# Later due times for part of the scaled inputs in the builder of a planned transformer block

## The chip, the cores and the metric

The kernel runs on one core of a Trainium2 chip. A core has TensorE (PE, matrix products into the PSUM banks), VectorE (DVE), ScalarE (ACT), GpSimd (POOL) and SyncE (SP, which issues most of the loads from memory). Each engine works through its own list of instructions in order and waits on semaphores for the others. The metric is device microseconds of one execution, as a median of runs.

## The reference

One block of a network on 256 tokens of width 2048, in float32: a gated feed-forward network (FFN), a mixer, and a second FFN, each between two RMS norms. Only the FFN matters here:

```python
def _rmsnorm(x, g):
    xf = x.astype(jnp.float32)
    y = xf * lax.rsqrt(jnp.mean(xf * xf, axis=-1, keepdims=True) + NORM_EPS)
    return (y * g.astype(jnp.float32)).astype(x.dtype)

def _swiglu(x, w_gate, w_up, w_down):
    return (jax.nn.silu(x @ w_gate) * (x @ w_up)) @ w_down
...
h = x
f = _swiglu(_rmsnorm(h, ln_ffn1_pre[l]), ffn1_gate[l], ffn1_up[l], ffn1_down[l])
h = h + MACARON_WEIGHT * _rmsnorm(f, ln_ffn1_post[l])
mx = _hybrid_mixer(...)
h = h + _rmsnorm(mx, ln_mix_post[l])
f = _swiglu(_rmsnorm(h, ln_ffn2_pre[l]), ffn2_gate[l], ffn2_up[l], ffn2_down[l])
h = h + MACARON_WEIGHT * _rmsnorm(f, ln_ffn2_post[l])
```

The hidden width of the FFN is 5632.

## The kernel before

**Products in three parts.** A float32 value v is kept as a high part H (a ScalarE cast to the type fp32r) and a low part L = v - H (a VectorE subtraction); `split` (line 651) makes both. A product of two such values is three matmuls, H.H, H.L and L.H (`mm3`, line 670). So each weight tile `w` that arrives needs a cast `wH` on ScalarE and a subtraction `wL` on VectorE before TensorE may use it. A weight pair is two k-tiles of 128 rows by 512 columns in one tile of 128x1024; it feeds 12 matmuls. There are five buffers each for `w`, `wH` and `wL`, given out in the order of the program; more are borrowed from 36 general units.

**Blocks of an FFN.** The 5632 hidden columns are worked in 11 blocks of 512, each with a gate half (banks `f`) and an up half (banks `l`), over 16 k-tiles of the input. Block 0 (banks `mm`) starts before the norm is known: it uses the raw input, and the norm is applied behind it. After block 0 `normed` (line 1221) makes the scaled inputs for blocks 2 and later. The input is held transposed in four quarters, i = 0 to 3, each of four k-tiles (128x1024). For each quarter `normed` does a multiplication by the norm's factors (in the first FFN in place, `xT<-xT,rsb`, after four column scalings `xT<-xT,cols` on ScalarE; in the second FFN `nx<-nx,rsb`, after an addition `nx<-xH,xL`), a `split` into `xH` and `xL`, and, for the first three quarters, `sums` (line 726): four small VectorE operations into `sf`, and a split of it into `sH` and `sL`. Block 1 still uses the raw input.

**Strassen-like blocks.** In blocks 2 to 10 some pairs of k-tiles ("quads", four or five of a block, from the first k-tiles on) are computed by a scheme with seven products in place of eight, which needs sums of inputs (`sums`) and sums of weights (VectorE: `t<-w,w`, `w<-w,t`). The first four products of each quad of block b + 1 (`early`, line 938) are woven into block b (`block_seq`, line 1088). In block 1 the first of them comes after seven of the eight gate pairs. It reads the first quarter; block 2's four quads read the first and second quarter and their sums; block 2's own pairs begin with the third quarter; the sums of the third quarter serve the fifth quad of block 3.

**The builder.** The program is recorded as a list of operations, and `Plan` (line 133) orders it: `deadlines` (line 292) gives each operation a due time, and `simulate` (line 328) plays the engines with modelled durations. Whenever an engine is free, it takes the ready operation with the earliest due time, or, if that one cannot get a buffer, the next. TensorE keeps the order of the program within each of its streams. The order that results is what is emitted. An operation is recorded with `nom`, the sum of the modelled times of the main matmuls recorded ahead of it, and with `lag`, 12000 ns unless something sets it:

```python
d = o.nom + (0.0 if o.eng == "PE" else o.lag) + soon.get(o.i, 0.0) * EASE
for x in o.succs:
    if o.eng == "PE" and x.eng == "PE":
        continue
    e = x.dl - o.dur - SYNC - (2500 if o.nbytes else 0)
    ...
    if e < d:
        d = e
o.dl = d
```

So an operation is due at its place in the program plus its lag, or a little before its earliest reader is due, whichever comes first. A matmul is due at its place; a weight low, therefore, just before its first matmul. All of `normed` is recorded between blocks 0 and 1, and so has the `nom` of the start of block 1.

In the profile nearly every instruction carries line 543, where the builder emits; instructions are told apart by the names of their tiles.

Of the kernel before, what the change touches and what calls it, by code (L numbers as in the profile page):

```python
# [88 lines left out]
NCOL = sum(n for _, n in COLS)  # L89
ONES = 8  # L90
FIRST = 0.4


class Op:
# [462 lines left out]
class Block:  # L557
# [68 lines left out]
    def raw(s, own=False):  # L626
        if own:
            return s.unit(p="w32")
        return s.tile(s.wp, [P, 1024], F32, "w32", "w32", W32_BUFS)
# [456 lines left out]
class Kernel(Block):  # L1086

    def block_seq(s, J, N, ev):
# [14 lines left out]
        if N and N.quads:  # L1103
            n, m = len(N.quads), len(own)
            a = FIRST if J.quads == [] else 0.0
            pos = [round((a + (1 - a) * (i + 0.5) / n) * (m - 3)) for i in range(n)]
# [114 lines left out]
    def normed(s, uT, rb, su, most, raw=None):  # L1221
        nc = s.nc
        V = nc.vector
        nT = s.new_T(len(uT))
        fl = lambda t: t.rearrange("p k t -> p (k t)")
        for i in range(len(uT)):
            (uH, uL), (nH, nL) = uT[i], nT[i]
            if raw:
                x = raw(i)
            else:  # L1230
                x = s.unit((P, 4, S), F32, "nx")
                with s.set(behind=s.late):
                    V.tensor_tensor(out=fl(x), in0=fl(uH).bitcast(F32),
                                    in1=fl(uL).bitcast(F32), op=ALU.add)
            V.tensor_tensor(out=x, in0=x, in1=rb.unsqueeze(1).to_broadcast([P, 4, S]),
                            op=ALU.mult)
            s.split(fl(x), fl(nH), fl(nL))
            if i < (most + 1) // 2:
                s.sums(x.rearrange("p (a b) (h t) -> p a b h t", a=2, h=2), su)
        return nT  # L1240

    def down(s, wd, at, KT, ev, raws, plan, q0=0, acc=()):
# [1039 lines left out]
```

## Time and profile before

| | |
|---|---|
| median of 3 runs | 1980.72 us (1979.87 to 1981.63) |
| the profiled execution | 1982.55 us |
| its span, first to last instruction | 1980.9 us |
| mean granted TensorE clock | 0.998 |
| busy: PE, DVE, ACT, POOL | 1967.8, 1828.3, 1279.1, 179.1 us |
| HBM read, written | 472.59 MB, 27.13 MB |

All times in the views count from the first instruction. A timeline row is start, duration, engine, line, operation, out<-in, shapes and count; in brackets the engine's idle time before it and what ended that. A matmul's duration is longer than its step to the next one, since matmuls are pipelined: the pace is read from the starts. A windows row gives a stretch, its length, the busy time (and instruction count) of PE, PEld, DVE, ACT and POOL, the granted clock, the DMA share and GB/s. A waits row is who waited for whom, the total in us, how many times, and the longest.

### The profile page before, as it was taken

The numbers are of one execution on the slowest core, as the hardware profiler recorded it, in microseconds if no ns is written. First come the engines' busy times: TensorE is split into PE (matmuls) and PEld (weight loads), VectorE is DVE, ScalarE is ACT, GpSimd is POOL, SyncE is SP. The second block draws the span as 40 slices with busy tenths as digits, with TensorE's granted clock in tenths as the row PEclk, the third lists the DMA queues.
The fourth block names the chain that finished last, engine by engine and source line by source line (L and its number), as shares of the span: only waits on it lengthen the run. The fifth ranks groups of instructions, "written<-read, shape, count | busy, mean of one in ns | idle before, by whom it ended". The sixth has DMA issues, their size and how long they took to land.

```text
span 1980.9 us, 28671 instructions
## 1 busy us (share of the span) xinstructions
PE 1967.8 (99%) x9650; PEld 1625.8 (82%) x9650; DVE 1828.3 (92%) x2313; ACT 1279.1 (65%) x1664; POOL 179.1 (9%) x260
## 2 busy tenths in 40 slices
PE   9999999999999999999999999999999999999998
PEld 7788888888888888888888788888888888888886
DVE  7999999999999988999799779998999999999996
ACT  8567767666655657764665465576667676766563
POOL 0111111100001020001400100011101111000000
PEclk9999999999999999999999999999999999999999
DMA  9899999987769788758566498778999999877684
GB/s 322 251 306 281 290 296 294 296 283 229 241 203 294 245 254 281 219 166 256 171 209 180 120 324 269 228 262 245 298 277 298 285 298 285 282 238 232 215 288 144
DMA packets 278163, 502.69 MB, mean 254 GB/s; under 512 B 25472, under 2 KB 53888, under 8 KB 278016
## 3 DMA queue, kind: packets, MB, share of 16 engines
q1 hardware_dynamic: 257360, 460.08, 70.1%
q0 software_dynamic: 20224, 40.38, 10.5%
q8 instruction: 76, 1.25, 0.2%
q14 instruction: 71, 0.58, 0.1%
q10 hardware_dynamic: 432, 0.40, 0.1%
HBM read 472.59 MB, written 27.13 MB: 252 GB/s over the span
## 4 chain that ended last, share of the span: by engine, by line
PE 59%; DVE 2%; ACT 1%; issue 1%; DMA 0%; POOLq 0%; ACTq 0%; DVEq 0%
PE l L543 18%; PE mm L543 18%; PE f L543 16%; PE p L543 4%; DVE wL L543 1%; PE pY L543 0%; PE pA L543 0%; ACT wH L543 0%; PE pU L543 0%; DVE AR L543 0%; PE pSa L543 0%; DVE BK L543 0%; PE mc L543 0%; PE pg L543 0%; PE pM L543 0%
## 5 line engine op out<-in xcount | busy, mean ns | idle before, releaser
L543 ACT CAST wH<-w 128x1024 fp32r<-128x1024 f32 (+2 forms) x730 | 749.8, 1043 | 450.3 <-PE mm L543 96.0
L543 DVE TENSOR_TENSOR wL<-w,wH 128x1024 fp32r<-128x1024 f32 (+2 forms) x730 | 870.3, 1208 | 89.1 <-ACT wH L543 76.1
L543 PE MATMUL l<-wL,xH 128*128 128x512 f32 x814 | 316.9, 389 | 0.2 <-DVE wL L543 0.2
L543 PE MATMUL l<-wH,xL 128*128 128x512 f32 x814 | 316.7, 389 | 0.0
L543 PE MATMUL l<-wH,xH 128*128 128x512 f32 x814 | 316.7, 389 | 0.0
L543 PE MATMUL mm<-wL,xH 128*128 128x512 f32 (+1 forms) x568 | 220.2, 388 | 1.3 <-DVE wL L543 1.3
L543 PE MATMUL mm<-wH,xH 128*128 128x512 f32 (+1 forms) x568 | 221.0, 389 | 0.2 <-ACT xH L543 0.2
L543 PE MATMUL mm<-wH,xL 128*128 128x512 f32 (+1 forms) x568 | 219.1, 386 | 0.0
L543 PE MATMUL f<-wL,xH 128*128 128x512 f32 x552 | 216.1, 392 | 2.9 <-DVE wL L543 2.9
L543 PE MATMUL f<-wH,xL 128*128 128x512 f32 x552 | 216.0, 391 | 0.0
L543 PE MATMUL f<-wH,xH 128*128 128x512 f32 x552 | 215.8, 391 | 0.0
L543 ACT CAST wH<-t 128x1024 fp32r<-128x1024 f32 (+1 forms) x166 | 169.4, 1020 | 62.5 <-DVE t L543 25.7
L543 DVE TENSOR_TENSOR wL<-t,wH 128x1024 fp32r<-128x1024 f32 (+1 forms) x166 | 195.9, 1180 | 5.9 <-ACT wH L543 4.8
L543 PEld LDWEIGHTS l<-wL,xH 128*128 128x128 f32 x814 | 152.8, 188 | 32.3 <-DVE wL L543 0.7
L543 PEld LDWEIGHTS l<-wH,xH 128*128 128x128 f32 x814 | 152.8, 188 | 31.7
L543 PEld LDWEIGHTS l<-wH,xL 128*128 128x128 f32 x814 | 152.8, 188 | 31.6
L543 DVE TENSOR_TENSOR t<-w,w 128x1024 f32<-128x1024 f32 (+1 forms) x112 | 134.4, 1200 | 1.4 <-DMA w<-in_w_in_dram 0.4
L543 PEld LDWEIGHTS mm<-wL,xH 128*128 128x128 f32 x568 | 106.9, 188 | 22.4 <-DVE wL L543 2.0
L543 PEld LDWEIGHTS mm<-wH,xH 128*128 128x128 f32 x568 | 106.7, 188 | 22.3 <-ACT xH L543 0.6
L543 PEld LDWEIGHTS f<-wL,xH 128*128 128x128 f32 x552 | 104.3, 189 | 25.0 <-DVE wL L543 3.3
L543 PEld LDWEIGHTS mm<-wH,xL 128*128 128x128 f32 x568 | 106.7, 188 | 20.5
L543 PEld LDWEIGHTS f<-wH,xH 128*128 128x128 f32 x552 | 104.3, 189 | 21.8
(324 smaller groups left out, 3095.7 us busy)
## 6 DMA issues: line engine op xcount, KB each, us to landing
w<-in_ffn_gate_dram SPq DMA_DIRECT2D x260, 256.0 KB, 6.0
w<-in_w_in_dram SPq DMA_DIRECT2D x120, 512.0 KB, 4.5
w<-in_ffn_down_dram SPq DMA_DIRECT2D x96, 512.0 KB, 4.8
w<-in_ffn_up_dram SPq DMA_DIRECT2D x92, 512.0 KB, 6.6
w<-in_ffn_gate_dram SPq DMA_DIRECT2D x88, 512.0 KB, 6.6
w<-in_ffn_up_dram SPq DMA_DIRECT2D x168, 256.0 KB, 5.9
w<-in_ffn_down_dram SPq DMA_DIRECT2D x152, 256.0 KB, 4.1
cx<-T SPq DMA_DIRECT2D x33, 512.0 KB, 4.1
```

What stands on the lines that cost most here:

```text
L543: ins = o.fn(*[real(x) for x in o.a], **{n: real(x) for n, x in o.k.items()})
```

## The change

Two tables of four lags, one for each quarter. `normed` sets the builder's lag to `NORM_LAG[i]` for all operations of quarter i, and to `SUM_LAG[i]` for its sums, and restores the old lag at the end. The first two quarters keep 12000 ns; the third and fourth get 40000 ns, and the sums 60000 ns. Both FFNs call `normed`. What is computed stays the same; the order of all engines but TensorE is planned anew from the due times.

```diff
 ONES = 8
 FIRST = 0.4
+NORM_LAG = 12000.0, 12000.0, 40000.0, 40000.0
+SUM_LAG = 12000.0, 12000.0, 60000.0, 60000.0
...
         nT = s.new_T(len(uT))
+        old = s.plan.lag
         fl = lambda t: t.rearrange("p k t -> p (k t)")
         for i in range(len(uT)):
+            s.plan.lag = NORM_LAG[i]
             (uH, uL), (nH, nL) = uT[i], nT[i]
             if raw:
                 x = raw(i)
...
             s.split(fl(x), fl(nH), fl(nL))
             if i < (most + 1) // 2:
-                s.sums(x.rearrange("p (a b) (h t) -> p a b h t", a=2, h=2), su)
+                with s.set(lag=SUM_LAG[i]):
+                    s.sums(x.rearrange("p (a b) (h t) -> p a b h t", a=2, h=2), su)
+        s.plan.lag = old
         return nT
```

## The prediction

> **What bounds the kernel now.** I read the page's span and busy shares first, then the table of waits of TensorE.
>
> ```profile
> span 1980.9 us, 28671 instructions
> PE 1967.8 (99%) x9650; PEld 1625.8 (82%) x9650; DVE 1828.3 (92%) x2313; ACT 1279.1 (65%) x1664; POOL 179.1 (9%) x260
> ```
> ```profile
> PE f L543 <- DVE wL L543: 2.9, 1, 2.9
> PE mm L543 <- DVE wL L543: 2.0, 3, 0.8
> ```
>
> TensorE is the bound, and almost nothing holds it up: it is busy 99% of the span. The work that it must do does not change here, so the time can move only by its waits. One of them is far longer than any other, 2.9 us for a weight low (wL, from VectorE) in front of an f matmul. The timeline of TensorE places it: the first row is the start of block 1, the others lie around the wait.
>
> ```profile
> 51.09 0.39 PE L543 MATMUL f<-wH,xH 128*128 128x512 f32 x1
> ...
> 64.69 0.39 PE L543 MATMUL f<-wH,xH 128*128 128x512 f32 x1
> 67.94 0.79 PE L543 MATMUL f<-wL,xH 128*128 128x512 f32 x1 [2.85 <-DVE wL L543]
> 68.53 0.63 PE L543 MATMUL f<-wH,xL 128*128 128x512 f32 x1
> 68.95 0.63 PE L543 MATMUL f<-wH,xH 128*128 128x512 f32 x1
> ...
> 75.89 0.39 PE L543 MATMUL f<-wH,xL 128*128 128x512 f32 x1
> 76.12 0.39 PE L543 MATMUL l<-wH,xH 128*128 128x512 f32 x1
> ```
> ```profile
> 68.00:70.00 2.00, 2.00 (x5) 1.61 (x6) 2.00 (x2) 0.00 (x0) 0.00 (x0) 0.50 0.43 61
> ...
> 74.00:76.00 2.00, 2.00 (x10) 1.60 (x9) 2.00 (x3) 1.76 (x3) 0.00 (x0) 0.99 0.42 161
> ```
>
> From 51.09 to 64.69 lie 60 matmuls, 0.2267 us each. From 64.69 to 76.12 lie 24 steps, which at that pace take 5.44 us and took 11.43. So this place costs **5.99 us**: 67.94 - 64.69 - 0.23 = 3.02 is the wait, and the other 2.97 is the slow stretch behind it, where the windows (busy times of PE, PEld, DVE, ACT, POOL, then the granted clock, the DMA share and GB/s) show the clock at 0.50, back at 0.99 from 74, and the rows step by 0.43 instead of 0.23.
>
> What VectorE did meanwhile, from its timeline:
>
> ```profile
> 47.63 2.35 DVE L543 TENSOR_TENSOR xT<-xT,rsb 128x1024 f32<-128x1024 f32 x2
> ...
> 54.56 1.21 DVE L543 TENSOR_TENSOR wL<-w,wH 128x1024 fp32r<-128x1024 f32 x1
> 55.70 1.09 DVE L543 TENSOR_TENSOR sf<-sf,xT 128x256 f32<-128x256 f32 x3
> ...
> 58.05 0.42 DVE L543 TENSOR_TENSOR sf<-xT 128x256 f32<-128x256 f32 x1
> 58.38 0.42 DVE L543 TENSOR_TENSOR sf<-xT,sf 128x256 f32<-128x256 f32 x1
> 58.72 1.22 DVE L543 TENSOR_TENSOR xL<-xT,xH 128x1024 fp32r<-128x1024 f32 x1
> 59.85 1.22 DVE L543 TENSOR_TENSOR sL<-sf,sH 128x1024 fp32r<-128x1024 f32 x1
> ...
> 66.67 1.22 DVE L543 TENSOR_TENSOR wL<-w,wH 128x1024 fp32r<-128x1024 f32 x1
> 67.80 1.22 DVE L543 TENSOR_TENSOR t<-w,w 128x1024 f32<-128x1024 f32 x1
> ```
>
> Between the weight lows of 54.56 and 66.67 VectorE worked 10.97 us without a gap, only on the scaled inputs and their sums (xT, sf, sL, xL): that run is what TensorE waited for. The late low starts the moment it ends, and was otherwise ready. ScalarE had made its high halves long before:
>
> ```profile
> 51.04 2.00 ACT L543 CAST wH<-w 128x1024 fp32r<-128x1024 f32 x2
> ...
> 70.83 1.04 ACT L543 CAST wH<-w 128x1024 fp32r<-128x1024 f32 x1 [10.38 <-issue]
> ```
>
> The order has its reason in the due times. A low is due about when its first matmul is due; the scaled inputs, made at the start of block 1, were due 12 us after it. A weight pair is 12 matmuls, 2.72 us, so the sixth pair starts 13.6 us into the block (51.09 + 13.6 = 64.69, the row above). Its low is the first one due behind all of that work.
>
> **The change, part by part.** No instruction is added or removed. For the third and fourth quarter of the inputs the due times move from 12 to 40 us, and the sums of the third to 60 us (the fourth has none). Moved on VectorE: two of the four scalings xT<-xT,rsb, two of the four xL, a third of the sf operations (4 of 12), one of three sL. By the rows' steps (47.63: 2.35 for two, less 1.21 for the last, is 1.14 each; 58.05 to 58.38, 0.335 each; 58.72 to 59.85, 1.135) that is 2.28 + 1.34 + 2.27 + 1.14 = **7.03 us**. On ScalarE: eight column scalings, two xH and one sH. No DMA and no POOL instruction is moved by a due time of its own; those behind them in the order move forward.
>
> *The late low.* If all 7.03 us leave the front of it, it starts at 59.64 and ends at 60.86; TensorE comes to it at 64.69 + 0.23 = 64.92. If only what lies behind 54.56 counts (two xL, one sL, three sf, 4.41 us), it ends at 63.48, still 1.4 us early. From both ends the wait is gone: -3.02 us, and the slow stretch with it, -2.97.
>
> *What is late next.* The following weight work on VectorE moves forward by 7.03 us too, and TensorE comes to it 5.99 earlier, so each margin grows by 1.04. The smallest now, after the stall, is that of the first l group:
>
> ```profile
> 72.41 1.22 DVE L543 TENSOR_TENSOR wL<-w,wH 128x1024 fp32r<-128x1024 f32 x1
> 73.55 1.22 DVE L543 TENSOR_TENSOR wL<-t,wH 128x1024 fp32r<-128x1024 f32 x1
> ```
>
> The first ends at 73.63 and its first use is the matmul behind 76.12, at 76.35: a margin of 2.7, which becomes 3.8. This needs data in time: VectorE did not idle before t<-w,w at 67.80, so its weights had landed, but not how early. If they came 2.7 us or less before 67.80, VectorE would wait, and could lose up to the whole 3.8; below that nothing is lost. I take nothing: ScalarE's cast at 70.83 had itself stood idle 10.38 us behind this VectorE work.
>
> *SyncE and its queue.* The next load after the late low waits for it, since it reuses the buffer that it frees:
>
> ```profile
> 67.96 7.68 SPq L543 DMA_DIRECT2D w<-in_ffn_up_dram  x4
> ```
>
> It goes out up to 7 us earlier; the DMA share of 0.43 at 68 to 70 shows room behind. POOL's next accumulating load waits for a ScalarE copy and moves with it. I cost both at nothing; the cover is the margin above.
>
> *The deferred work.* It must go somewhere: 4.55 us (scalings and xL) by 40 us into the block, 91, and 2.48 (sf, sL) by 111. Idle VectorE time behind the stall:
>
> ```profile
> 80.00:100.00 20.00, 20.00 (x90) 16.58 (x89) 16.90 (x17) 13.88 (x17) 3.54 (x4) 1.00 0.71 218
> 100.00:120.00 20.00, 20.00 (x90) 16.57 (x89) 20.00 (x23) 13.46 (x18) 1.49 (x5) 1.00 1.03 330
> ```
>
> 3.1 us are free between 80 and 100, none between 100 and 120. With the 1.04 of margin won, 4.55 - 3.1 - 1.04 = 0.4 us is not covered at 100 and 2.9 at 120, at worst. Between 100 and 140 ScalarE waited 2.5 us for TensorE to free a weight buffer, so there the halves were ahead by all the buffers:
>
> ```profile
> ACT wH L543 <- PE l L543: 2.5, 1, 2.5
> ```
>
> So the margin absorbs it: bound 0 to 2.9 us lost, I take 0. The third quarter is first read by block 2, after 192 matmuls of block 1 and 48 of early products (240 x 0.2267 = 54.4, at 105.5), 14 us behind its new due time.
>
> *The second FFN* has the same code, and no such wait:
>
> ```profile
> 1360.00:1380.00 20.00, 20.00 (x90) 16.57 (x89) 14.82 (x14) 12.44 (x13) 1.72 (x2) 1.00 0.85 249
> ```
>
> Its scaled inputs were made before block 1 began; now up to 7.03 + 2.27 us (two nx additions) may fall behind 1340, into 5.2 us of idle VectorE time between 1360 and 1380. No gain, and nothing lost as long as a low is ahead by some 4 us. It also shows what the first FFN looks like without the stall: 20.00 of 20 on PE in block 1.
>
> **The sum.** -3.02 - 2.97 = -5.99 us. Against the profiled execution, 1982.55 (span 1980.9), that is 1976.6. The median of the runs is 1980.72, 1.8 below the profiled one; I take the difference off the median: **1974.7**.
>
> [...] The windows put the clock at 0.50 after a wait of 3.02 us. [...]
>
> **Rivals.**
> (a) The timed runs had no slow stretch, only the profiled one did. Two other waits for a low cost no clock: 0.77 us at 17.74 stands in a window at 1.00. For it: the fastest run, 1979.87, lies 2.68 under the profiled one, nearly the 2.97. Against: the runs shown differ by 1.76 in any case, and nothing makes them differ in order or load. Then 1980.72 - 3.02 = 1977.7.
>
> ```profile
> 17.74 0.50 PE L543 MATMUL mm<-wL,xH 128*128 128x512 f32 x1 [0.77 <-DVE wL L543]
> 16.00:18.00 2.00, 1.24 (x5) 0.65 (x5) 1.54 (x2) 1.93 (x4) 0.00 (x0) 1.00 1.06 398
> ```
>
> (b) A short wait of 1 to 3 us remains, at the l group or between 100 and 140 (bounds above), with no fall of the clock: 1975.7 to 1977.7.
> (c) The deferred work lands as one lump. At 40 us into the block it goes ahead of lows due later, as now at 12 us, and 4.55 to 7.03 us beat their margin. The price of such a stall is the one seen, 5.99. In the first FFN alone it cancels the gain: 1980.7. In the second as well (near 1380, where up to 6.8 us fall due) it gives 1986.7: the slower case. It decides where the margin of a low is under the lump; for it, VectorE at 20.00 of 20 from 100 to 120; against it, the lump is smaller than the 10.97 us of now, split into two due times, and lies where VectorE has idle time.
> (d) The change does nothing: were a reader of the third quarter due early, it would pull the due times forward again. Its first reader comes 54 us into the block, so I give this little. 1980.7.
>
> **How the numbers follow.** My forecast 0.68; (a) 0.08; (b) 0.10; (c) cancelled 0.05, slower 0.06; (d) 0.03. The forecast with its spread (runs differ by about 0.9 to each side, and shorter waits of 2.0 us in all may come or go) spans 1973.0 to 1976.7; with (a) and (b) the range is 1973.0 to 1978.6, holding 0.86. About 0.2%, 4.0 us, is what a measurement can tell from no change: faster is below 1976.76. Faster: 0.68 + 0.05 of (b) = 0.73. Same: (a), the rest of (b), (c) cancelled, (d) = 0.21. Slower 0.06.
>
> **What would show it.** Right: no wait of f for wL in the table of waits; block 1 at some 90 matmuls for each 20 us from 60 to 80 and a clock of 1.00 there; two xL and one sL behind 80 instead of before 67; the span down by 6. Wrong: a new PE wait near 70 (data late), between 90 and 140, or near 1380 (the lump), or a wait near 65 that is merely shorter.

## The result: faster by 4.6 us, and the profile after

| | before | changed |
|---|---|---|
| median of the runs | 1981.13 us (16 runs, 1979.69 to 1982.12) | 1976.55 us (16 runs, 1975.96 to 1978.34) |
| ratio, 95% interval | | 0.9978 (0.9970 to 0.9986) |
| the profiled execution | 1982.55 | 1976.51 |
| its span | 1980.9 | 1974.8 |

Forecast were 1974.7 us and 5.99 us less; the median fell by 4.6 us, the span of the two profiles by 6.1. The changed kernel once more, later, gave 1976.66 against 1981.09, 0.9976 (0.9967 to 0.9985).

The page's head and the whole table of TensorE's waits in the changed kernel:

```profile
span 1974.8 us, 28657 instructions
PE 1964.8 (99%) x9650; PEld 1622.9 (82%) x9650; DVE 1827.2 (93%) x2313; ACT 1279.0 (65%) x1664; POOL 179.0 (9%) x260
```
```profile
PE mm L545 <- DVE wL L545: 2.0, 3, 0.8
PE warm L545 <- POOL ident masks.py:199: 1.5, 1, 1.5
PE po L545 <- ACT dg L545: 1.4, 1, 1.4
PE pk L545 <- DVE nb L545: 0.2, 1, 0.2
```

The wait of f for wL is gone, and no other has come. TensorE's timeline around the place (block 1 begins at 51.34 here, so 64.94 is its sixth pair), and VectorE's:

```profile
51.34 0.39 PE L545 MATMUL f<-wH,xH 128*128 128x512 f32 x1
...
64.94 0.39 PE L545 MATMUL f<-wH,xH 128*128 128x512 f32 x1
65.16 0.39 PE L545 MATMUL f<-wL,xH 128*128 128x512 f32 x1
...
70.38 0.39 PE L545 MATMUL l<-wH,xH 128*128 128x512 f32 x1
70.60 0.39 PE L545 MATMUL l<-wL,xH 128*128 128x512 f32 x1
```
```profile
58.87 1.22 DVE L545 TENSOR_TENSOR wL<-w,wH 128x1024 fp32r<-128x1024 f32 x1
60.01 1.22 DVE L545 TENSOR_TENSOR t<-w,w 128x1024 f32<-128x1024 f32 x1
...
64.02 1.22 DVE L545 TENSOR_TENSOR xT<-xT,rsb 128x1024 f32<-128x1024 f32 x1
65.15 1.22 DVE L545 TENSOR_TENSOR wL<-w,wH 128x1024 fp32r<-128x1024 f32 x1
...
69.16 1.21 DVE L545 TENSOR_TENSOR xT<-xT,rsb 128x1024 f32<-128x1024 f32 x1
...
82.86 1.21 DVE L545 TENSOR_TENSOR xL<-xT,xH 128x1024 fp32r<-128x1024 f32 x1
...
85.16 1.22 DVE L545 TENSOR_TENSOR xL<-xT,xH 128x1024 fp32r<-128x1024 f32 x1
```

The low that was late ends at 60.09, 5.1 us ahead of its use at 65.16. From the first f to the first l matmul TensorE takes 19.04 us, 84 steps of 0.2267, where it took 25.03. The first l group's low ends at 66.37 and is used at 70.60, a margin of 4.2. The deferred scalings stand at 64.02 and 69.16 and the deferred xL at 82.86 and 85.16, singly between weight lows; the sums follow from 91 to 97.

The windows show where VectorE paid for it, and that TensorE did not notice:

```profile
60.00:80.00 20.00, 20.00 (x90) 16.57 (x89) 20.00 (x21) 14.85 (x18) 0.87 (x1) 1.00 1.06 327
80.00:100.00 20.00, 20.00 (x90) 16.57 (x89) 19.68 (x23) 15.06 (x18) 3.49 (x4) 1.00 0.89 262
100.00:120.00 20.00, 20.00 (x90) 16.55 (x89) 19.87 (x22) 12.14 (x14) 2.26 (x5) 1.00 0.90 302
```

VectorE's third number fills from 16.90 of 20 to 19.68 between 80 and 100; the granted clock is 1.00 throughout.

### The profile page after: what moved, and what is told of

It is laid out like the page before. It is cut to its first block, busy times and chain, and to the rows that moved or that the text cites. A ratio compares the mean times of both kernels' runs of the same rounds, so it can differ in the third digit from the quotient of the medians.

```text
span 1974.8 us, 28657 instructions
## 1 busy us (share of the span) xinstructions
PE 1964.8 (99%) x9650; PEld 1622.9 (82%) x9650; DVE 1827.2 (93%) x2313; ACT 1279.0 (65%) x1664; POOL 179.0 (9%) x260
## 4 chain that ended last, share of the span: by engine, by line
PE 96%; DVE 2%; ACT 1%; DMA 1%; issue 1%; SPq 0%; POOLq 0%; ACTq 0%; DVEq 0%
PE l L545 34%; PE f L545 30%; PE mm L545 22%; PE p L545 6%; DMA w<-in_ffn_gate_dram 1%; DVE wL L545 0%; PE pY L545 0%; PE pA L545 0%; ACT wH L545 0%; PE tr L545 0%; PE pU L545 0%; DVE AR L545 0%; PE pSa L545 0%; DVE BK L545 0%; PE mc L545 0%
## 5 line engine op out<-in xcount | busy, mean ns | idle before, releaser
L545 PEld LDWEIGHTS f<-wH,xL 128*128 128x128 f32 x552 | 103.6, 188 | 21.5
```

What stands on the lines that cost most here:

```text
L545: ins = o.fn(*[real(x) for x in o.a], **{n: real(x) for n, x in o.k.items()})
```

## The experiments

All kernels keep the order of TensorE's matmuls, so the start of each can be set against that of the same matmul in the changed kernel's profile. "Lead-in" is the time from the first f to the first l matmul, 19.04 us without a stall; "delay" is that start less the changed kernel's, at four places of its time axis. The median is over the timed runs, the rest from one profile each; that of ffn1_only lies above all its other runs (1978.85), that of sum_only below them (1975.83).

| kernel | median, us | lead-in | delay at 51 | at 80 | at 435 | at the end |
|---|---|---|---|---|---|---|
| before | 1981.13 | 25.03 | -0.2 | 5.8 | 5.5 | 6.1 |
| before_again | 1981.25 | 23.61 | -0.1 | 4.5 | 4.3 | 4.3 |
| ffn1_only | 1976.83 | 19.04 | -0.2 | -0.2 | 0.7 | 2.3 |
| ffn2_only | 1981.62 | 23.80 | -0.7 | 4.0 | 3.8 | 4.8 |
| sum_only | 1977.38 | 19.04 | -0.7 | -0.7 | -0.9 | -0.7 |
| norm_only | 1977.55 | 19.04 | 0.3 | 1.2 | 1.0 | 1.3 |
| q4_only | 1982.36 | 19.92 | -0.3 | 2.9 | 5.2 | 5.8 |
| lag20 | 1982.26 | 19.04 | 0.4 | 2.6 | 3.7 | 6.3 |
| fill5 | 1980.67 | 19.72 | 0.5 | 3.0 | 4.3 | 4.4 |
| fill6 | 1980.44 | 20.90 | -0.2 | 3.8 | 3.6 | 4.7 |
| fill7 | 1981.78 | 23.66 | -0.4 | 4.9 | 4.7 | 5.6 |
| fill10 | 1985.96 | 27.44 | 1.1 | 9.5 | 9.6 | 10.8 |
| after_again | 1976.66 | 19.04 | -0.5 | -0.5 | -0.5 | -0.1 |

### Why 6.1 in the profiles and 4.6 in the medians: the kernel before, again

No edit.

> The kernel before, unchanged, against itself. Open: the two profiled spans differ by 6.1 us (1980.9 and 1974.8), the medians by only 4.6 (1981.13 and 1976.55). [...] Rival A (the stretch is always there, and the changed kernel loses 1.4 us elsewhere): every run has the clock of 0.998 and a stretch of 2.97 us; median 1981.1 as well.

Its median was 1981.25, ratio 1.0001 (0.9992 to 1.001). Its profile has the same wait, and a shorter slow stretch; the last row is from the first profile of this kernel, for comparison:

```profile
64.83 0.39 PE L543 MATMUL f<-wH,xH 128*128 128x512 f32 x1
68.06 0.80 PE L543 MATMUL f<-wL,xH 128*128 128x512 f32 x1 [2.85 <-DVE wL L543]
```
```profile
66.00:68.00 2.00, 0.00 (x0) 0.00 (x0) 2.00 (x3) 0.00 (x0) 0.00 (x0) 0.93 0.33 76
68.00:70.00 2.00, 1.94 (x5) 1.57 (x6) 2.00 (x3) 0.00 (x0) 0.00 (x0) 0.50 0.38 82
70.00:72.00 2.00, 2.00 (x8) 1.63 (x7) 2.00 (x4) 1.04 (x2) 0.00 (x0) 0.72 0.90 339
```
```profile
66.00:68.00 2.00, 0.07 (x1) 0.07 (x1) 2.00 (x3) 0.00 (x0) 0.00 (x0) 0.80 0.38 86
```

A window of 2 us that shows 0.93 holds 0.28 us of half clock, one that shows 0.72 holds 1.12: 0.28 + 2.0 + 1.12 = 3.4 us of half clock, against some 6.8 in the first profile (0.50 from about 67.2 to 74). The lead-in is 23.61: a stall of 4.57 us, 3.00 of wait and 1.57 of clock. Of four profiles with this stall (before, before_again, ffn2_only, fill7) three have the short stretch, with 4.57, 4.76 and 4.62 us in all, and one the long one, with 5.99. So rival A's fixed stretch of 2.97 us falls: the price varies from execution to execution. That the short stretch is the common one rests on three profiles of four and on the medians, which differ by just its 4.6 us. No profile is without a stretch; a timed run without one is not excluded.

If the price varies, the times of the runs may go in steps with their mean clock. The eleven runs of before_again do not show that (six at 0.998 with a median of 1980.88, five at 0.999 with 1981.28). The 33 runs of the same kernel that were timed beside them do: 1981.31 for the 23 at 0.998, 1980.5 for the ten at 0.999.

### One FFN at a time

```diff
-            s.plan.lag = NORM_LAG[i]
+            s.plan.lag = NORM_LAG[i] if raw else old        # ffn1_only; "if not raw": ffn2_only
...
-                with s.set(lag=SUM_LAG[i]):
+                with s.set(lag=SUM_LAG[i] if raw else old):
```

> The new due times in the first FFN alone; the second FFN keeps 12 us. My theory: the whole gain sits in the stall near 65 us of the first FFN: 1976.6, like the changed kernel. Rival A (the second FFN gives back 1.4 us of a gain of 6.0): 1975.1.

> The new due times in the second FFN alone. My theory: no gain and no loss, the stall of 3.0 us stays: 1981.1. Rival A: 1982.5, with a new wait or a lost margin behind 1340 us. A gain here would say that the second FFN had a wait that the profile does not show.

The first gave 1976.83, 0.998 (0.9971 to 0.9988): the whole gain. The second gave 1981.62, 1.0004 (0.9995 to 1.0013), with the wait still in place: no gain, and no loss that can be measured. Rival A, by which the second FFN gives back 1.4 us, falls: the 1975.1 that it asks of ffn1_only lies below that kernel's interval.

### Which of the deferred work counts

Three kernels defer a part: sum_only the sums of the third quarter, norm_only the scalings and splits (all but the third quarter's scaling, which its sums still need early), q4_only the fourth quarter.

```diff
 # sum_only
-NORM_LAG = 12000.0, 12000.0, 40000.0, 40000.0
+NORM_LAG = 12000.0, 12000.0, 12000.0, 12000.0
 # norm_only
-SUM_LAG = 12000.0, 12000.0, 60000.0, 60000.0
+SUM_LAG = 12000.0, 12000.0, 12000.0, 12000.0
 # q4_only: SUM_LAG as in norm_only, and
-NORM_LAG = 12000.0, 12000.0, 40000.0, 40000.0
+NORM_LAG = 12000.0, 12000.0, 12000.0, 40000.0
```

> Only the sums of the third quarter get a later due time (60 us); the scalings and splits of the third and fourth quarter keep 12 us. That takes 1.34 + 1.14 = 2.48 us out of the 10.97 us run in front of the late low. My theory: the wait of 3.02 shrinks to 0.5 and the clock does not fall: 1981.1 less 4.1 (of the 4.6 measured) = 1977.0. Rival C (any wait at this place costs the clock too): a slow stretch of 1.6 to 3 us stays: 1978.6 to 1980.0. Rival (what is late next): with the stall gone TensorE comes 5 us earlier to the first l group, whose weight lows moved forward by only 2.48 of it with a margin of 2.7: a second wait of up to 0.2 us there.

> Only the scalings and splits of the third and fourth quarter get 40 us; the sums of the third quarter keep 12 us, and so their source, the scaling of the third quarter, does too. That takes one scaling and two xL, 3.41 us, out of the run in front of the late low. My theory (any VectorE time counts alike): the wait of 3.0 is gone by 0.4. Next, the first l group: its margin was 2.7, TensorE comes up to 6.0 earlier, its lows 3.4, and in the order of this kernel the deferred scaling stands just ahead of it (1.14): a wait of 0 to 1.0 us there, no clock fall; 1976.6 to 1977.7. Rival D (the sums are what counts): 1981.1, with the wait still there.

> Only the fourth quarter, which has no sums, gets 40 us: one scaling and one xL, 2.27 us less in front of the late low. My theory: a wait of 0.75 us remains there, without a fall of the clock; then TensorE comes 5.2 us earlier to the l group, whose lows come 1.1 earlier (the scaling stands again ahead of them) with a margin of 2.7: a second wait of about 1.4 us. In all 2.2 us: 1978.8. Rival E (only the low that was named counts): 0.75, so 1977.4. Rival C (any wait here costs the clock): 1980.5 or more.

sum_only: 1977.38, 0.9984 (0.9975 to 0.9993), and no wait at all in its head, where 0.5 us was expected. norm_only: 1977.55, 0.9984 (0.9975 to 0.9993); its only wait there is the one foreseen at the l group:

```profile
PE l L545 <- DVE wL L545: 0.3, 1, 0.3
```

So rival D falls: either part alone removes the stall, since each brings the low about 3.5 us forward (from the start of block 1 it starts 3.42 us earlier in norm_only and 3.57 in sum_only). sum_only did better than its 2.48 us allow, because VectorE no longer stood idle while it waited for a high half near 44. ScalarE's two copies `rsb<-rb`, which the first scaling `xT<-xT,rsb` needs, came 4 to 5 us earlier, and that scaling fills the gap. VectorE and ScalarE in the kernel before, then in sum_only:

```profile
44.22 1.22 DVE L543 TENSOR_TENSOR wL<-w,wH 128x1024 fp32r<-128x1024 f32 x1 [0.75 <-ACT wH L543]
45.37 1.22 DVE L543 TENSOR_TENSOR xT<-xT,rsb 128x1024 f32<-128x1024 f32 x1
44.09 0.42 ACT L543 COPY rsb<-rb 128x128 f32<-128x128 f32 x2
```
```profile
41.62 1.22 DVE L545 TENSOR_TENSOR xT<-xT,rsb 128x1024 f32<-128x1024 f32 x1
42.76 2.35 DVE L545 TENSOR_TENSOR wL<-w,wH 128x1024 fp32r<-128x1024 f32 x2
39.03 0.26 ACT L545 COPY rsb<-rb 128x128 f32<-128x128 f32 x1
```

The copies come early (39 to 41) in sum_only, lag20 and the changed kernel, all of which put the sums off. They stay at 44 to 45 in the kernel before, norm_only and q4_only. It is not the column scalings on ScalarE that make the room: sum_only leaves them where they were, and norm_only, which puts off those of the fourth quarter, keeps the idle time (0.70 us). Why the builder moves the copies when the sums are late is not shown. In the changed kernel VectorE's idle time between 40 and 45 is gone in the same way, first the kernel before, then the changed one:

```profile
40.00:45.00 5.00, 5.00 (x24) 4.14 (x23) 4.13 (x4) 4.89 (x9) 0.00 (x0) 1.00 1.05 406
```
```profile
40.00:45.00 5.00, 5.00 (x24) 4.14 (x23) 5.00 (x6) 5.00 (x8) 0.00 (x0) 1.00 1.05 408
```

That is 0.87 us more of VectorE in front of the low. The prediction had not counted it: it forecast the low 7.03 us earlier; measured from the start of block 1 it came 66.67 - 51.09 - (58.87 - 51.34) = 8.05 earlier.

q4_only: 1982.36, 1.0009 (1.0000 to 1.0017): not the 1978.8 of my theory. The number alone lies within rival C's 1980.5 or more, but rival C needs a fall of the clock, and this profile has none (granted clock 1.00 from 60 to 82). Its waits between 60 and 90, and then between 395 and 430:

```profile
PE l L545 <- DVE wL L545: 1.7, 2, 1.1
PE f L545 <- DVE wL L545: 0.6, 1, 0.6
```
```profile
PE l L545 <- DVE sg L545: 0.7, 1, 0.7
PE l L545 <- DVE wL L545: 0.5, 1, 0.5
```

The wait at the sixth pair cost 0.74 us by TensorE's starts, as expected, with no fall of the clock, and two further waits came at the l groups: 3.2 us were lost in the head (delay from -0.3 to 2.9) where 2.2 was expected. Another 2.3 us went at 390 to 425 (2.9 to 5.2), and 0.6 near 1700. These later losses my theory does not have. Why the order built for this kernel is tighter there is not settled.

### The lump brought near

```diff
-NORM_LAG = 12000.0, 12000.0, 40000.0, 40000.0
-SUM_LAG = 12000.0, 12000.0, 60000.0, 60000.0
+NORM_LAG = 12000.0, 12000.0, 20000.0, 20000.0
+SUM_LAG = 12000.0, 12000.0, 20000.0, 20000.0
```

> The lump of the prediction's rival (c), brought near: the same work is deferred, but all of it to 20 us, sums included. The late low goes ahead, and the 7.03 us stand behind it, around the lows of the first early products (70 to 73 us), whose margin in the changed kernel is about 3.8. My theory: the lump beats the margin, a wait or several of 3.3 us in all between 70 and 76 in place of the one at 65; with one slow window of the clock (1.7) 1981.6, without 1979.9. Rival F (a later due time is enough, wherever it lies, because VectorE has idle time behind): 1976.6.

1982.26, 1.0009 (1.0000 to 1.0018): the whole gain is gone, and rival F with it. The waits between 60 and 90, and VectorE's lump between two weight lows:

```profile
PE f L545 <- DVE wL L545: 1.1, 1, 1.1
PE l L545 <- DVE wL L545: 0.5, 1, 0.5
```
```profile
69.12 1.23 DVE L545 TENSOR_TENSOR xL<-xT,xH 128x1024 fp32r<-128x1024 f32 x1
70.25 1.23 DVE L545 TENSOR_TENSOR sL<-sf,sH 128x1024 fp32r<-128x1024 f32 x1
71.39 1.23 DVE L545 TENSOR_TENSOR xL<-xT,xH 128x1024 fp32r<-128x1024 f32 x1
72.52 1.23 DVE L545 TENSOR_TENSOR t<-w,w 128x1024 f32<-128x1024 f32 x1
73.66 1.23 DVE L545 TENSOR_TENSOR wL<-w,wH 128x1024 fp32r<-128x1024 f32 x1
```

The head lost 2.2 us (0.4 to 2.6) where 3.3 was expected. The rest came later: 1.1 us at 412 to 425, 1.1 near 750, and 1.5 in the second FFN, near 1700. My theory has none of these, and what makes them is not settled; the median lies above both its numbers. The late low itself is on time here (lead-in 19.04). So a due time that only just clears the one low moves the queue behind it: the prediction's rival (c) is a real mechanism, worth 2.2 us here, and at 40 and 60 us nothing of it shows.

### VectorE's time alone, in doses

The changed kernel with n multiplications more on VectorE, due like the work that was moved away. Nothing reads their result.

```diff
         s.plan.lag = old
+        if raw:
+            dm = s.unit((P, 4, S), F32, "dm")
+            for _ in range(5):                               # 6, 7, 10
+                V.tensor_tensor(out=dm, in0=rb.unsqueeze(1).to_broadcast([P, 4, S]),
+                                in1=rb.unsqueeze(1).to_broadcast([P, 4, S]), op=ALU.mult)
         return nT
```

> The changed kernel with five multiplications of 128x1024 on VectorE more (they compute nothing that is read), due 12 us into block 1 like the work that was taken away: 5 x 1.135 = 5.7 us in front of the late low, whose margin is now 4.9 (it ends at 60.1, TensorE comes near 65.0). My theory (VectorE time in front of that low is the cause, whatever it computes): a wait of 0.8 us near 65, and one of about 1.1 at the l group, whose margin of 3.8 is eaten too; no clock fall: 1978.5. Rival G (the cause was the buffers or loads that the deferred tiles held, not VectorE's time): 1976.6, or 1976.6 plus nothing that lies near 65.

> As with five, but six idle multiplications, 6.8 us against a margin of 4.9: a wait of 1.9 us near 65 by my theory. [...]

> Seven idle multiplications, 7.9 us against a margin of 4.9: a wait of 3.0 us near 65, the stall of the kernel before made anew. My theory: the slow stretch comes back with it, one or two windows of 3.4 us (1.6 to 3.0 us lost): 1981.2 to 1982.7. Rival G (buffers or loads were the cause): 1976.6.

> Ten idle multiplications, 11.35 us against a margin of 4.9: a wait of 6.4 us near 65. [...] Theory K (the loss grows with the wait, 1 us of clock for 1 us of wait): 6.4 + 6.4, 1989.4.

| | expected wait near 65 | measured (start to start, less 0.23) | half clock behind it |
|---|---|---|---|
| fill5 | 0.8 | 0.55 | none |
| fill6 | 1.9 | 1.7 | none |
| fill7 | 3.0 | 2.9 | some 3.4 us |
| fill10 | 6.4 | 6.5 | some 6.8 us, 3.0 of it within the wait |

TensorE's row and the clock behind it, for six, seven and ten:

```profile
66.74 0.50 PE L545 MATMUL f<-wL,xH 128*128 128x512 f32 x1 [1.57 <-DVE wL L545]
```
```profile
68.00:70.00 2.00, 2.00 (x10) 1.68 (x9) 2.00 (x3) 0.36 (x1) 0.00 (x0) 1.00 0.96 330
```
```profile
67.67 0.50 PE L545 MATMUL f<-wL,xH 128*128 128x512 f32 x1 [2.70 <-DVE wL L545]
```
```profile
68.00:70.00 2.00, 2.00 (x7) 1.54 (x6) 2.00 (x3) 0.00 (x0) 0.00 (x0) 0.57 1.06 255
70.00:72.00 2.00, 2.00 (x7) 1.57 (x6) 2.00 (x3) 1.48 (x2) 0.00 (x0) 0.58 0.73 246
```
```profile
72.69 0.80 PE L545 MATMUL f<-wL,xH 128*128 128x512 f32 x1 [6.31 <-DVE wL L545]
```
```profile
70.00:72.00 2.00, 0.00 (x0) 0.00 (x0) 2.00 (x3) 0.00 (x0) 0.00 (x0) 0.50 0.27 68
74.00:76.00 2.00, 2.00 (x6) 1.52 (x6) 2.00 (x3) 0.46 (x1) 0.00 (x0) 0.50 0.91 305
```

The dose makes the wait, within 0.3 us at every step, with operations that hold one buffer and read nothing new. Rival G (buffers or loads) falls. fill7 is the kernel before made anew: 1981.78, 1.0002 (0.9993 to 1.0011). fill10, at 1985.96, lies far from theory K (1989.4): its lead-in grew by 8.4 us, the wait of 6.5 and 1.9 more. fill5 came out 2.2 us over what I expected, at 1980.67, and fill6 at 1980.44: the short waits at the l groups were larger (fill5 lost 2.5 us in the head, expected 1.9; fill6 3.9, of which its lead-in has 1.9), and fill5 lost 1.2 more at 412 to 425. So the medians of these two do not follow the dose; the wait near 65 does. Rival C of sum_only and q4_only, by which any wait at this place costs the clock, falls with fill6 as well: its granted clock is 1.00 behind a wait of 1.7 us.

### The changed kernel, again

No edit.

> The changed kernel, unchanged, once more. Open: the kernel with the new due times in the first FFN alone has the same order of instructions there, and yet its profile lost 0.8 us at 412 to 425 us, in short waits of l and f for weight lows, that the changed kernel's own profile does not have. Theory M (the margin there is about nothing in this order, and small differences of a run decide): a loss of 0 to 1 us there, not the same as in the first profile or by chance the same; median 1976.6, with the head (block 1 from its first f to its first l matmul in 19.04 us) unchanged. Rival N (the second FFN's order reaches back, by loads that are built ahead): no loss there, as in the first profile.

Its profile has no loss at 412 to 425 (delay -0.5 before and behind), as in the first one. So that ffn1_only lost 0.8 us there, in one profile that lies 2 us above its median, is left open between the two theories; its median is 0.2 to 0.3 us above the changed kernel's, less than the intervals can tell.

## Why the prediction was right, and what was mis-sized

**The wait.** Right: -3.02 was forecast, and the wait is gone with nothing in its place. The cause was VectorE's time in front of one weight low; the doses, sum_only and norm_only show it from three sides.

**The slow stretch.** The term of the sum that was mis-sized. It stood at 2.97, read from one profiled execution, and three of four profiles with the same stall have 1.57 to 1.8. With that the sum is 3.0 + 1.6 = 4.6, the measured difference. The forecast of 1974.7 missed by 1.85 us: 1.4 is this term, and the other 0.4 is the base, three runs with a median of 1980.72 where sixteen gave 1981.13. The prediction had noted that the profiled run lay 1.8 us above the median and took the difference off the median all the same; the two profiled executions of this kernel differ by 1.75, and 1.4 of that is the longer stretch. Rival (a), timed runs with no slow stretch at all, was the wrong form of the right doubt: each of the four profiles with this wait has the stretch, three of them at half the length (3.4 us of half clock against 6.8).

**What is late next.** Right: a margin of 3.8 was forecast for the first l group, 4.2 measured. The data came in time.

**The deferred work.** Right in that 2.9 us of lost margin at worst were absorbed. It did not wait for its due time: the scalings stand at 64 and 69, where the builder had nothing ready that was due sooner.

**The second FFN.** Right: ffn2_only is the same as before within its interval. In the changed kernel most of the second FFN's scaled inputs are still made ahead of block 1 (the four nx multiplications lie at 1308.8 to 1330.4), since VectorE has time for them there.

**The other side.** Rival (c) did not happen at 40 and 60 us. At 20 us it does (lag20), by short waits, 2.2 us in the head in all, rather than one of 3 with its clock (granted clock 1.00 from 60 to 82).

## What to carry to other kernels

In a queue ordered by due times, a batch of work due together can stand as one block in front of a single item due just behind it; give the parts that are needed late their own due time, past the stretch in which the queue has no slack, and not just past the one item that was late. Price a stall from several profiles when part of its cost is a lowered clock: the wait was 2.9 to 3.0 us each time, the half clock behind it 3.4 us or 6.8, the cost in all 4.6 to 4.8 or 6.0. An edit to the recorded operations or their due times also plans the whole kernel anew: in their profiles q4_only, lag20 and fill5 lost 1.4 to 3.7 us more behind the head, far from what was edited. And where the matmuls keep their order, the delay of the same matmul between two kernels shows where each microsecond was lost: in the kernel before, 6.0 of 6.3 us in the head (-0.2 to 5.8 to 6.1).

## What the runs showed of the hardware

The half clock that came with a wait lasted about 3.4 us in three profiles (before_again, ffn2_only, fill7) and about 6.8 in two (before, fill10). The waits were 2.9 to 3.0 us in the first four of the table below and 6.5 in fill10; after waits of up to 1.7 us (fill5 0.55, q4_only 0.74, fill6 1.7) the granted clock stayed at 1.00. Between 1.7 and 2.9 us no run shows where the fall begins.

The profiles also bear on why 3.4 us or 6.8: the clock fell at a different place of the wait, or behind it, in each execution. All in us:

| profile | TensorE idle | clock falls at | idle before the fall | idle behind it | half clock |
|---|---|---|---|---|---|
| before | 65.1 to 67.9 | 67.2 | 2.1 | 0.7 | 6.8 |
| before_again | 65.2 to 68.1 | 67.7 | 2.5 | 0.4 | 3.4 |
| ffn2_only | 64.6 to 67.4 | 67.6 | 2.8 | none | 3.4 |
| fill7 | 65.0 to 67.7 | 68.3 | 2.7 | none | 3.4 |
| fill10 | 66.4 to 72.7 | 69.7 | 3.3 | 3.0 | 6.8 |
| fill6 | 65.2 to 66.7 | no fall | 1.6 in all | | none |

Where TensorE stood idle for 0.7 us or more behind the fall, the half clock lasted 6.8 us; where it stood 0.4 us or less, 3.4. By this reading the same wait cost 6.0 us or 4.6 according to where in it the clock fell. Five falls fit it, and no run set the place of the fall, so it is a reading of these traces and not a shown cause; what sets the place is not shown.
